# A transformer block on one Trainium2 core: the up weights of two chunks split by transfers instead of by engines, and 24 products into an unread bank at the end

## The chip, the cores and the metric

One core of a Trainium2 chip runs the whole program. The metric is device microseconds of one execution, here the median of the runs; the profile is of one more execution, and its times are counted from its first instruction.

## The reference

One layer: attention, then a feed-forward block with squared ReLU, each between two RMS norms, on 256 tokens of width 1024 in float32. The change touches the feed-forward block alone.

```python
def squared_relu_mlp(x, w_up, w_down):
    return jnp.square(jax.nn.relu(x @ w_up)) @ w_down

h = h + rms_norm(moba_attention(rms_norm(h, g1), w_qkv, w_o), g2)
u = squared_relu_mlp(rms_norm(h, g3), w_up, w_down)      # w_up [1024, 4096], w_down [4096, 1024]
h = h + rms_norm(u, g4)
```

## The kernel before

**Split weights.** Every float32 weight is split into two float32r parts, hi (rounded to 12 bits) and lo (the rest, weight minus hi). A product of float32 matrices is three products of parts (`mm3`, L209 to L214): hi by hi (L212), hi by lo (L213) and lo by hi (L214). In the up products the weight is the stationary operand: L212 and L213 use its hi part, L214 its lo part.

**The stream of pieces.** `Weights` (L28 to L99) cuts all weights into 48 pieces of 128 partitions by 2048 columns (1 MB) in the order of their use. Here the pieces that matter are, by number: up2 22 and 23, down1 24 and 25, up3 26 and 27, down2 28 and 29, up4 30 and 31, down3 32 and 33, up5 34 and 35. `load` (L45) issues one load into one of five raw buffers from the SP queue. `pump` (L71) splits: for one of the four steps of a piece ACT writes a quarter of hi (L83) and DVE the same quarter of lo (L84). Each of the tags whi and wlo has four buffers, so that piece i takes the parts buffer of piece i-4, and a step of piece i is only emitted when piece i-4 has been marked as used up by `done` (L75). When a piece's four steps are emitted, the next load is emitted.

**The feed-forward block.** For chunks c from 1 to 7 the loop at L669 runs `up_chunk(c)` (L645: four groups f of 24 products, eight row blocks k by three, 128x128 by 128x256; piece `up{c}` holds k 0 to 3 and its successor k 4 to 7) and `down_chunk(c - 1)` (L659: 48 products of 128x128 by 128x512). After each f two steps are pumped (L656, L667). The steps of an up piece begin to be emitted at the end of `up_chunk(c - 1)` (L655, L656).

**Order.** TensorE (PE) and the SP queue keep the order of the program (L113). ACT, DVE and POOL are put in order by the framework's scheduler, which goes by priority and by when it expects an operand to be ready; on the chip each engine then works strictly in that order. The last chunk's `down` products go by token tile, each followed by its norm and its two output transfers (L679 to L686).

Of the kernel before, what the change touches and what calls it, by code (L numbers as in the profile page):

```python
# [8 lines left out]
F32 = mybir.dt.float32  # L9
F32R = mybir.dt.float32r  # L10
BF16 = mybir.dt.bfloat16
AF = mybir.ActivationFunctionType
ALU = mybir.AluOpType
# [4 lines left out]
P = 128  # L18
HEADS = 8
EPS = 1e-6  # L20
# [5 lines left out]


class Weights:  # L28
    """Streams the weights through SBUF in pieces of [128, 2048] and splits each float32
    exactly into two float32r parts: hi (12 bits, rounded) and lo (the rest). A piece is split  # L30
    in four steps; step (i, j) is the j-th of piece i."""

    N = 2048

    def __init__(self, nc, raw_pool, part_pool, raw_bufs, part_bufs):
        self.nc, self.raw_pool, self.part_pool = nc, raw_pool, part_pool
        self.raw_bufs, self.part_bufs = raw_bufs, part_bufs
        self.sources, self.raw, self.parts, self.steps, self.split = [], {}, {}, [], set()
        self.loaded = self.finished = self.next = self.part = 0

    def add(self, src, how, cuts=1):
        self.sources.append((src, how, cuts))
        return len(self.sources) - 1

    def load(self, n=None):  # L45
        """The next n parts of a piece's load, by default all that remain."""
        i = self.loaded
        if i >= len(self.sources):
            return
        src, _, cuts = self.sources[i]  # L50
        k, c = src.shape[1], src.shape[2]
        if i not in self.raw:
            self.raw[i] = self.raw_pool.tile([P, k, c], F32, name=f"raw{i}", tag="raw", bufs=self.raw_bufs)
        n = n or cuts - self.part
        w = k // cuts
        for j in range(self.part, self.part + n):
            self.nc.sync.dma_start(self.raw[i][:, j * w:(j + 1) * w, :], src[:, j * w:(j + 1) * w, :])
        self.part += n
        if self.part == cuts:
            self.loaded += 1  # L60
            self.part = 0
# [9 lines left out]
    def pump(self, n, lo_engine=None):  # L71
        nc = self.nc
        while n > 0 and self.next < len(self.steps):
            i, j = self.steps[self.next]
            if i >= self.finished + self.part_bufs or i >= self.loaded:  # L75
                return
            if i not in self.parts:
                shape = list(self.raw[i].shape)
                self.parts[i] = [self.part_pool.tile(shape, F32R, name=f"w{p}{i}", tag=f"w{p}", bufs=self.part_bufs)
                                 for p in ("hi", "lo")]  # L80
            hi, lo = (self.slice(t, i, j) for t in self.parts[i])
            x = self.slice(self.raw[i], i, j)
            nc.scalar.activation(hi, x, AF.Copy)  # L83
            (lo_engine or nc.vector).tensor_tensor(lo, x, f32(hi), op=ALU.subtract)  # L84
            self.split.add((i, j))
            self.next += 1
            n -= 1
            if sum((i, q) in self.split for q in range(4)) == 4:
                self.load()
# [13 lines left out]
def block(ctx: ExitStack, tc: tile.TileContext, x, g_mix_pre, g_mix_post, g_ffn_pre, g_ffn_post,  # L103
          w_up, w_down, w_qkv, w_o, out):
    nc = tc.nc
    S, D = x.shape[1], x.shape[2]
# [12 lines left out]
    at = ctx.enter_context(tc.tile_pool(name="at", bufs=4, space=PSUM))  # L119

    def bank(pool, name):
        return pool.tile([P, 512], F32, name=name, tag="b")

    # ---- the weights in the order of their use
    wq = w_qkv[0].rearrange("(k p) c -> p k c", p=P)
    wo = w_o[0].rearrange("(k p) c -> p k c", p=P)
    wu = w_up[0].rearrange("(k p) c -> p k c", p=P)
# [2 lines left out]
    piece = {}  # L130

    def add_cols(name, w, c, how, cuts=1):
        """512 columns in two pieces of four row blocks"""
        i = piece[name] = W.add(w[:, 0:4, c:c + 512], how, cuts)
        W.add(w[:, 4:8, c:c + 512], how, cuts)
        if how == "cols":
            W.steps += [(i + e, j) for j in range(4) for e in range(2)]
        else:
            W.steps += [(i + e, j) for e in range(2) for j in range(4)]

    def add_rows(name, w, k):
        """four row blocks in two pieces"""
        i = piece[name] = W.add(w[:, k:k + 2, :], "rows")
        W.add(w[:, k + 2:k + 4, :], "rows")
        W.steps += [(i + e, j) for e in range(2) for j in range(4)]
# [10 lines left out]
    for c in range(NC):  # L156
        add_cols(f"up{c}", wu, 512 * c, "cols" if c else "k")
        if c > 0:
            add_rows(f"down{c - 1}", wd, 4 * (c - 1))
    add_rows(f"down{NC - 1}", wd, 4 * (NC - 1))  # L160

    # ---- loads: x's columns as the first weights need them
    xs = const.tile([P, NT, D], F32, name="xs")
    xv = x[0].rearrange("(t p) d -> p t d", p=P)
    grow = [const.tile([KT, P], F32, name=f"grow{i}") for i in range(2)]
# [15 lines left out]
    for name, g in (("mix", g_mix_post), ("ffn", g_ffn_post)):  # L181
        gb[name] = const.tile([P, D], F32, name=f"g_{name}")

    # ---- constants
    ident = const.tile([P, P], F32, name="ident")
    make_identity(nc, ident)
    one = const.tile([P, P], F32, name="one")
# [2 lines left out]
    nc.gpsimd.tensor_copy(ones, one)  # L190
    power = const.tile([P, 2], F32, name="power")
    nc.gpsimd.memset(power, -0.5)
    # distances of queries 128.. to keys 0..255, then of queries 0.. to keys 0..127
    dist = const.tile([P, 384], F32, name="dist")
    nc.gpsimd.iota(dist[:, 0:256], pattern=[[-1, 256]], base=P, channel_multiplier=1,
                   allow_small_or_imprecise_dtypes=True)
# [10 lines left out]
    oT = [const.tile([P, HEADS, S], F32R, name=f"oT{i}") for i in range(2)]  # L207

    def mm3(ps, a, b, start, stop):  # L209
        """ps (+)= (a0 + a1).T @ (b0 + b1) without the product of the low parts, which lies below  # L210
        a float32's rounding."""
        nc.tensor.matmul(ps, lhsT=a[0], rhs=b[0], start=start, stop=False)  # L212
        nc.tensor.matmul(ps, lhsT=a[0], rhs=b[1], start=False, stop=False)  # L213
        nc.tensor.matmul(ps, lhsT=a[1], rhs=b[0], start=False, stop=stop)  # L214
# [7 lines left out]
        nc.vector.scalar_tensor_tensor(dst[1], ps, scale, f32(dst[0]), op0=ALU.mult, op1=ALU.subtract)  # L222

    def square(junk, x, acc):
        """acc = the row sums of x * x / D"""
        nc.scalar.activation(junk, x, AF.Square, scale=D ** -0.5, accum_out=acc)

    def rstd_of(a, b, dst):
        """dst = (a + b + EPS) ** -0.5"""
        ms = small.tile(list(dst.shape), F32, name="ms")  # L230
        nc.vector.scalar_tensor_tensor(ms, a, EPS, b, op0=ALU.add, op1=ALU.add)
        nc.gpsimd.tensor_tensor(dst, ms, power[:, :dst.shape[1]], op=ALU.pow)

    def diag_of(rstd):
        """diagonal matrices of rstd, split in two parts"""
        dg = [small.tile([P, S], F32R, name=f"diag{i}", bufs=1) for i in range(2)]
        for t in range(NT):
            hi, lo = (a[:, t * P:(t + 1) * P] for a in dg)
            nc.vector.tensor_scalar(hi, ident, rstd[:, t:t + 1], None, op0=ALU.mult)
            nc.vector.scalar_tensor_tensor(lo, ident, rstd[:, t:t + 1], f32(hi), op0=ALU.mult, op1=ALU.subtract)  # L240
        return dg

    def row_of(dg, dst, pool):
        """dst[:, t] = rstd[t] on every partition"""
        ps = bank(pool, "psrow")
        for i in range(2):
            nc.tensor.matmul(ps[:, :S], lhsT=ones, rhs=dg[i], start=i == 0, stop=i == 1)
        nc.scalar.activation(dst, ps[:, :S], AF.Copy)

    # ---- x transposed, times the first gain; its rows' norms come in later  # L250
    banks = [bank(at, f"xt{j}") for j in range(4)]

    def transpose_x(k, t):
# [87 lines left out]
        nc.scalar.activation(hi, full, AF.Copy)  # L341
        nc.vector.tensor_tensor(lo, full, f32(hi), op=ALU.subtract)

    # ---- attention, a head at a time; the queries of the second half come first
    prob, probT = {}, {}
    cut = ((0, 256, 1), (256, 384, 0))

# [54 lines left out]
        W.pump(1, nc.gpsimd if h % 2 else None)  # L402
        (q_evac if kind == "q" else k_evac)(h, ps)

    # ---- values, queries and keys of the first heads
    idle = const.tile([P, 512], BF16, name="idle")
    psi = bank(mm, "psidle")

    def keep_busy(n):
        """products of zeros, which keep TensorE's clock up while it waits"""  # L410
        for _ in range(n):
            nc.tensor.matmul(psi, lhsT=idle[:, :P], rhs=idle, start=True, stop=True)

# [67 lines left out]
        if h == 3:  # L481
            transpose_p(4)

    # ---- projection of the heads' outputs
    acc = [[bank(mm, f"acc{t}_{c}") for c in range(2)] for t in range(NT)]

    def rows_unit(name, j, act, t, c, start, stop):
# [17 lines left out]
            transpose_p(h + 5)  # L505
        attend(h + 4)

    # ---- h = x + rms_norm(attention), over x; then transposed, times the next gain
    qk_pool.release()
    mlp = ctx.enter_context(tc.tile_pool(name="mlp", bufs=2, reuse_waits="tile"))  # L510
    yg = mlp.tile([P, NT, D], F32, name="yg", bufs=1)

    class PostNorm:
        """residual + rms_norm of a token tile of the accumulated rows"""

        def __init__(self, t, name):
            self.t, self.gain = t, gb[name]
# [21 lines left out]
            if late is not None and f == 0:  # L539
                late()  # L540

    # ---- the feed-forward block
    ssq2 = const.tile([P, 2, NT], F32, name="ssq2")
    rstd2 = const.tile([P, NT], F32, name="rstd2")
    rrow2 = const.tile([P, S], F32, name="rrow2")
# [11 lines left out]
        nc.scalar.activation(u, r, AF.Square)  # L557
        nc.vector.tensor_tensor(lo, u, f32(hi), op=ALU.subtract)  # L558

    # the first chunk goes by token tiles, its result being transposed: the first tile's products  # L560
    # run while the second one's norm is worked out
    rT = {}

    def up_first(t, k):
# [114 lines left out]
    for t in range(NT):  # L679
        norm = PostNorm(t, "ffn")  # L680
        for c in range(2):
            last_rows(f"down{NC - 1}", act_down, t, c)
            norm.take(c)
        for a, b in ((0, 512), (512, D)):
            norm.put(yg, a, b)
            nc.sync.dma_start(ov[:, t, a:b], yg[:, t, a:b])  # L686
    W.done(2)


# [23 lines left out]
```

## Time and profile before

| | us |
|---|---|
| median of 2 runs | 307.49 (306.96 to 308.01) |
| span of the profiled execution | 304.8 |
| PE busy in it | 295.1 (97%) |
| DVE busy | 194.1 (64%) |
| ACT busy | 166.6 (55%) |
| POOL busy | 24.4 (8%) |

The span runs from the first to the last instruction that the profiler recorded; the run's time is 2.7 us longer. A product that PE runs is shown with the time from its start to its modelled end, and these overlap: the pace of products is read from one start to the next. In a timeline a line is start, duration, engine, line of the kernel, operation, output<-input and count, and in brackets the idle time of the engine before it and what ended it.

### The profile page before, as it was taken

Reading aid. Unit: us, or ns where it says so; the run is one execution under the profiler, and the core shown is the slowest. Engines: PE = TensorE matmul, PEld = TensorE weight load, DVE = VectorE, ACT = ScalarE, POOL = GpSimd, SP = SyncE. Lnnn points to the kernel's source line nnn. Section 1 sums busy time; section 2 is a strip of 40 time slices with the busy share of each in tenths; the row PEclk is TensorE's granted clock in tenths of the full one; section 3 lists DMA queues with packets and bytes.
Section 4 is the critical chain, followed back from the end, with each engine's and each line's share of the span. In section 5 each row is a group of like instructions: output and inputs, shape, how many; then the busy total and the mean of one; then the engine's idle time right before and its main releaser. Section 6 shows DMA issues by size and latency. Waiting matters only on the chain.

```text
span 304.8 us, 4862 instructions
## 1 busy us (share of the span) xinstructions
PE 295.1 (97%) x1838; PEld 261.9 (86%) x1838; DVE 194.1 (64%) x403; ACT 166.6 (55%) x395; POOL 24.4 (8%) x38
## 2 busy tenths in 40 slices
PE   8999999999999989999999999999999999999991
PEld 4689999988998868898898898898898898898880
DVE  3569989774688296899448447447447447547042
ACT  4777938765393365987437427427527526526020
POOL 4000224002200072000000000000000000000000
PEclk9999999999999999999999999999999999999998
DMA  6998694739405234078970860960960950300012
GB/s 201 374 387 310 205 380 172 251 133 347 141 3 166 110 138 140 0 254 293 298 261 1 310 245 0 326 226 2 336 214 9 345 199 12 129 0 3 0 57 80
DMA packets 22055, 53.79 MB, mean 176 GB/s; under 512 B 1024, under 2 KB 1552, under 8 KB 22032
## 3 DMA queue, kind: packets, MB, share of 16 engines
q1 hardware_dynamic: 22032, 53.49, 50.1%
q8 instruction: 14, 0.23, 0.3%
q14 instruction: 9, 0.07, 0.1%
HBM read 52.44 MB, written 1.05 MB: 175 GB/s over the span
## 4 chain that ended last, share of the span: by engine, by line
PE 80%; issue 10%; DVE 5%; DMA 2%; SPq 1%; ACT 1%; POOL 1%; DVEq 0%; POOLq 0%
PE psu L212 10%; PE psu L214 10%; PE psu L213 10%; PE acd L213 9%; PE acd L212 9%; PE acd L214 9%; PE psq L212 3%; PE psq L213 3%; PE psq L214 3%; DVE wlo L84 2%; PE psv L292 2%; PE psv L294 2%; PE psv L296 2%; DMA raw<-in_attn_w_qkv_dram 2%; PE psk L212 1%
## 5 line engine op out<-in xcount | busy, mean ns | idle before, releaser
L84 DVE TENSOR_TENSOR wlo<-raw,whi 128x512 fp32r<-128x512 f32 x182 | 118.3, 697 | 43.2 <-ACT whi L83 43.0
L83 ACT ACTIVATE whi<-raw 128x512 fp32r<-128x512 f32 x192 | 107.0, 623 | 46.4 <-PE acd L214 33.3
L212 PE MATMUL psu<-xT,whi 128*128 128x256 f32 x224 | 63.4, 283 | 0.0
L213 PE MATMUL psu<-xT,whi 128*128 128x256 f32 x224 | 63.3, 282 | 0.0
L214 PE MATMUL psu<-xT,wlo 128*128 128x256 f32 x224 | 62.9, 281 | 0.0
L213 PE MATMUL acd<-wlo,uhi 128*128 128x512 f32 x128 | 50.5, 395 | 0.0
L212 PE MATMUL acd<-whi,uhi 128*128 128x512 f32 x128 | 50.5, 395 | 0.0
L214 PE MATMUL acd<-whi,ulo 128*128 128x512 f32 x128 | 50.5, 394 | 0.0
L214 PEld LDWEIGHTS psu<-xT,wlo 128*128 128x128 f32 x224 | 42.5, 190 | 0.0
L213 PEld LDWEIGHTS psu<-xT,whi 128*128 128x128 f32 x224 | 42.1, 188 | 0.3
L212 PEld LDWEIGHTS psu<-xT,whi 128*128 128x128 f32 x224 | 41.9, 187 | 0.3
L556 ACT ACTIVATE uhi<-r 128x256 fp32r<-128x256 f32 x28 | 11.6, 413 | 35.0 <-DVE r L555 35.0
L214 PEld LDWEIGHTS acd<-whi,ulo 128*128 128x128 f32 x128 | 24.1, 188 | 5.6
L212 PEld LDWEIGHTS acd<-whi,uhi 128*128 128x128 f32 x128 | 24.1, 188 | 5.4
L213 PEld LDWEIGHTS acd<-wlo,uhi 128*128 128x128 f32 x128 | 24.1, 189 | 5.3
L558 DVE TENSOR_TENSOR ulo<-u,uhi 128x256 fp32r<-128x256 f32 x28 | 11.8, 423 | 14.4 <-ACT u L557 14.4
L555 DVE SCALAR_TENSOR_TENSOR r<-psu,rrow 128x256 f32<-128x256 f32 x28 | 11.7, 419 | 13.7 <-PE psu L214 13.7
L212 PE MATMUL psq<-xT,whi 128*128 128x256 f32 x64 | 18.4, 288 | 0.0
L212 PE MATMUL psk<-xT,whi 128*128 128x256 f32 x64 | 18.4, 287 | 0.0
L529 POOL TENSOR_TENSOR rs<-mss,power 128x1 f32<-128x1 f32 x4 | 2.2, 550 | 198.6 <-DVE mss L527 198.6
L214 PE MATMUL psq<-xT,wlo 128*128 128x256 f32 x64 | 18.1, 282 | 0.0
L213 PE MATMUL psq<-xT,whi 128*128 128x256 f32 x64 | 18.0, 282 | 0.0
(121 smaller groups left out, 455.2 us busy)
## 6 DMA issues: line engine op xcount, KB each, us to landing
raw<-in_w_up_dram SPq DMA_DIRECT2D x16, 1024.0 KB, 5.6
raw<-in_w_down_dram SPq DMA_DIRECT2D x16, 1024.0 KB, 7.5
raw<-in_attn_w_qkv_dram SPq DMA_DIRECT2D x10, 1024.0 KB, 8.6
raw<-in_attn_w_o_dram SPq DMA_DIRECT2D x4, 1024.0 KB, 5.7
raw<-in_attn_w_qkv_dram SPq DMA_DIRECT2D x8, 256.0 KB, 6.3
out_dram<-yg SPq DMA_DIRECT2D x4, 256.0 KB, 2.0
xs<-in_x_dram SPq DMA_DIRECT2D x2, 256.0 KB, 4.9
xs<-in_x_dram SPq DMA_DIRECT2D x1, 512.0 KB, 7.1
```

Of the source, the lines that this page charges most:

```text
L83: nc.scalar.activation(hi, x, AF.Copy)
L84: (lo_engine or nc.vector).tensor_tensor(lo, x, f32(hi), op=ALU.subtract)
L212: nc.tensor.matmul(ps, lhsT=a[0], rhs=b[0], start=start, stop=False)
L213: nc.tensor.matmul(ps, lhsT=a[0], rhs=b[1], start=False, stop=False)
L214: nc.tensor.matmul(ps, lhsT=a[1], rhs=b[0], start=False, stop=stop)
L292: nc.tensor.matmul(psv[0][t], lhsT=x0[t], rhs=w[0], start=first, stop=False)
L294: nc.tensor.matmul(psv[0][t], lhsT=x1[t], rhs=w[0], start=False, stop=False)
L296: nc.tensor.matmul(psv[0][t], lhsT=x0[t], rhs=w[1], start=False, stop=last)
L529: nc.gpsimd.tensor_tensor(self.rs, ms, power[:, :1], op=ALU.pow)
L555: nc.vector.scalar_tensor_tensor(r, ps[:, :S], 0.0, rrow2, op0=ALU.max, op1=ALU.mult)
L556: nc.scalar.activation(hi, r, AF.Square)
L558: nc.vector.tensor_tensor(lo, u, f32(hi), op=ALU.subtract)
```

## The change

The two pieces each of up3 (26 and 27) and up5 (34 and 35) are marked (`W.rounded`). For a marked piece `load` issues nothing and only counts it as loaded. At its first step `pump` emits three things: a load of the whole 1 MB from memory into hi, issued from the POOL queue, which rounds on its way; one ACT instruction that writes lo as minus hi, 128x2048; and a second load of the same 1 MB from the POOL queue that adds onto lo. The other steps of the piece emit nothing. So lo becomes weight minus hi, and its ACT and DVE steps and its SP load are gone. At the very end of the program 24 products are emitted on PE into a bank that nobody reads: six each of bf16 zeros by 512 columns, of the last down piece's hi part read as bf16 by 512 columns, of the same as float32r by 512, and as float32r by 256 columns. The removed comments leave empty lines and change nothing.

```diff
@@ class Weights
+        self.rounded, self.started = set(), 0
+    def by_dma(self, i):
+        return i in self.rounded
     def load(self, n=None):
         src, _, cuts = self.sources[i]
+        if self.by_dma(i):
+            self.loaded += 1
+            return
@@ pump
             if i not in self.parts:
-                shape = list(self.raw[i].shape)
+                shape = list(self.sources[i][0].shape)
                 self.parts[i] = [self.part_pool.tile(shape, F32R, name=f"w{p}{i}", tag=f"w{p}", bufs=self.part_bufs)
                                  for p in ("hi", "lo")]
+            if self.by_dma(i):
+                if (i, -1) not in self.split:
+                    self.split.add((i, -1))
+                    (hi, lo), src = self.parts[i], self.sources[i][0]
+                    nc.gpsimd.dma_start(hi, src)
+                    nc.scalar.activation(lo, hi.bitcast(F32), AF.Copy, scale=-1.0)
+                    nc.gpsimd.dma_start(lo, src, accum_op=ALU.add)
+                self.split.add((i, j))
+                self.next += 1
+                n -= 1
+                if sum((i, q) in self.split for q in range(4)) == 4:
+                    self.load()
+                continue
             hi, lo = (self.slice(t, i, j) for t in self.parts[i])
@@ the list of pieces
         add_cols(f"up{c}", wu, 512 * c, "cols" if c else "k")
         if c > 0:
+            if c in (3, 5):
+                W.rounded |= {piece[f"up{c}"], piece[f"up{c}"] + 1}
             add_rows(f"down{c - 1}", wd, 4 * (c - 1))
@@ the end
+    tail = bank(at, "pstail")
+    hi, lo = W.parts[piece[f"down{NC - 1}"]]
+    for n, (a, b) in enumerate(((idle[:, :P], idle), (hi.bitcast(BF16)[:, 0, 0:P], hi.bitcast(BF16)[:, 1, 0:512]),
+                                (hi[:, 0, 0:P], hi[:, 1, 0:512]), (hi[:, 0, 0:P], hi[:, 1, 0:256]))):
+        for _ in range(6):
+            nc.tensor.matmul(tail[:, :b.shape[-1]], lhsT=a, rhs=b, start=True, stop=True)
     W.done(2)
```

## Rows read from the trace of the kernel before

**Rows 1.** The page: busy shares, then the chain that ended last, by engine.

```profile
PE 295.1 (97%) x1838; PEld 261.9 (86%) x1838; DVE 194.1 (64%) x403; ACT 166.6 (55%) x395; POOL 24.4 (8%) x38
...
PE 80%; issue 10%; DVE 5%; DMA 2%; SPq 1%; ACT 1%; POOL 1%; DVEq 0%; POOLq 0%
```

**Rows 2.** Timeline of PE, the end of up_chunk(2).

```profile
160.85 0.29 PE L213 MATMUL psu<-xT,whi 128*128 128x256 f32 x1
160.98 0.28 PE L214 MATMUL psu<-xT,wlo 128*128 128x256 f32 x1
...
162.42 0.28 PE L214 MATMUL psu<-xT,wlo 128*128 128x256 f32 x1
162.54 0.40 PE L212 MATMUL acd<-whi,uhi 128*128 128x512 f32 x1
162.77 0.40 PE L213 MATMUL acd<-wlo,uhi 128*128 128x512 f32 x1
```

**Rows 3.** Timeline of PE, the start of up_chunk(3).

```profile
173.69 0.28 PE L212 MATMUL psu<-xT,whi 128*128 128x256 f32 x1
173.81 0.29 PE L213 MATMUL psu<-xT,whi 128*128 128x256 f32 x1
173.93 0.30 PE L214 MATMUL psu<-xT,wlo 128*128 128x256 f32 x1
...
175.13 0.28 PE L212 MATMUL psu<-xT,whi 128*128 128x256 f32 x1
```

**Rows 4.** Timeline of ACT, from up_chunk(2) to the start of up_chunk(3).

```profile
161.18 2.72 ACT L83 ACTIVATE whi<-raw 128x512 fp32r<-128x512 f32 x5
163.80 0.40 ACT L556 ACTIVATE uhi<-r 128x256 fp32r<-128x256 f32 x1
164.11 0.40 ACT L557 ACTIVATE u<-r 128x256 f32<-128x256 f32 x1
164.41 1.66 ACT L83 ACTIVATE whi<-raw 128x512 fp32r<-128x512 f32 x3
168.32 2.19 ACT L83 ACTIVATE whi<-raw 128x512 fp32r<-128x512 f32 x4 [2.25 <-PE acd L214]
173.89 2.19 ACT L83 ACTIVATE whi<-raw 128x512 fp32r<-128x512 f32 x4 [3.37 <-PE acd L214]
```

**Rows 5.** The page's groups of the split: busy, mean ns, idle before.

```profile
L84 DVE TENSOR_TENSOR wlo<-raw,whi 128x512 fp32r<-128x512 f32 x182 | 118.3, 697 | 43.2 <-ACT whi L83 43.0
L83 ACT ACTIVATE whi<-raw 128x512 fp32r<-128x512 f32 x192 | 107.0, 623 | 46.4 <-PE acd L214 33.3
```

**Rows 6.** Timeline of DVE: the last lo parts of up3.

```profile
164.95 2.49 DVE L84 TENSOR_TENSOR wlo<-raw,whi 128x512 fp32r<-128x512 f32 x4
```

**Rows 7.** Transfers in 154.2 to 160.2, a load alone: rate in 40 slices, then issue to landing.

```profile
GB/s 382 355 300 109 82 27 27 27 137 191 150 164 109 96 205 191 205 273 328 328 423 437 423 423 355 423 423 369 396 355 259 178 191 55 14 0 0 0 0 0
...
raw<-in_w_up_dram SPq DMA_DIRECT2D x1, 1024.0 KB, 5.4
```

**Rows 8.** Transfers in 166 to 176, three loads that overlap: issue to landing.

```profile
raw<-in_w_down_dram SPq DMA_DIRECT2D x2, 1024.0 KB, 7.7
raw<-in_w_up_dram SPq DMA_DIRECT2D x1, 1024.0 KB, 5.6
```

**Rows 9.** Stretches: length, then busy us (count) of PE, PEld, DVE, ACT, POOL, clock, DMA share, GB/s.

```profile
160.00:170.00 10.00, 10.00 (x56) 8.59 (x55) 7.32 (x14) 7.30 (x16) 0.00 (x0) 1.00 0.17 46
172.00:173.00 1.00, 1.00 (x5) 0.78 (x5) 0.00 (x0) 0.00 (x0) 0.00 (x0) 1.00 1.05 430
```

**Rows 10.** Timeline of the SP queue, loads 30 to 33 and 34.

```profile
154.41 12.83 SPq L57 DMA_DIRECT2D raw<-in_w_up_dram  x2
167.47 4.41 SPq L57 DMA_DIRECT2D raw<-in_w_down_dram  x2
177.08 12.84 SPq L57 DMA_DIRECT2D raw<-in_w_up_dram  x2
```

**Rows 11.** The costliest POOL instruction of the split (groups by form).

```profile
L84 POOL TENSOR_TENSOR wlo<-raw,whi 128x512 fp32r<-128x512 f32 x10 | 14.0, 1413 | 36.6 <-ACT whi L83 36.5
```

**Rows 12.** Timeline of the end: the last product and the last issues of output.

```profile
297.98 0.40 PE L214 MATMUL acd<-whi,ulo 128*128 128x512 f32 x1
...
300.85 0.99 SPq L686 DMA_DIRECT2D out_dram<-yg  x2
```

**Rows 13.** Stretches after the last product, columns as in rows 9.

```profile
301.00:302.00 1.00, 0.00 (x0) 0.00 (x0) 0.49 (x1) 0.00 (x0) 0.00 (x0) 1.00 0.30 119
302.00:303.00 1.00, 0.00 (x0) 0.00 (x0) 0.00 (x0) 0.00 (x0) 0.00 (x0) 0.90 1.01 393
303.00:304.00 1.00, 0.00 (x0) 0.00 (x0) 0.00 (x0) 0.00 (x0) 0.00 (x0) 0.50 0.04 12
```

**Rows 14.** Timeline of PE at the program's start: bf16 products of zeros.

```profile
1.17 2.31 PE L412 MATMUL psidle<-idle 128*128 128x512 bf16 x5 [1.17 <-DVE idle L415]
```

## Prediction

> **What bounds the kernel now.** I read the busy shares and the chain of waits first [rows 1]: PE is busy for 97% of the span and carries 80% of the chain, the other engines have a third or more of it free. In the feed-forward block PE is paced by its own products: in the up products one starts every 0.12 us, in the down products every 0.23 us [rows 2, 3]. The reader should then look at who delivers to PE around the changed place, the start of up_chunk(3). Its pieces 26 and 27 are split by ACT in 161.18 to about 166.1 [rows 4] and by DVE until 164.95 + 2.49 = 167.44 [rows 6], while PE asks for them at 173.69 [rows 3]. So there are 6.2 us of slack, and faster splitting buys nothing. The same pattern returns in each chunk, 22.7 us apart, so what holds for up3 holds for up5. What counts is whether the new way still delivers by 173.7.
>
> **What is removed.** Four pieces lose four steps each: 16 ACT instructions of 0.623 us (10.0 us) and 16 DVE instructions of 0.697 us (11.2 us) [rows 5], and four SP loads. None lay on PE's path (6.2 us of slack), so I take 0 for all of it. A gain is excluded: PE starts a product at its pace without a hole on both sides of the seam [rows 2, 3].
>
> **What is added before up_chunk(3), and when it can start.** The rounding load of piece 26 writes a hi buffer that piece 22 held. Its last reader is the L213 product at 160.85, for lo the L214 at 160.98 [rows 2]; so it can go at about 161.2. Piece 27 takes piece 23's buffers, free after the product at 162.42, about 162.6. ACT's order speaks for it that waiting is for exactly this: five of the eight steps of these pieces start at 161.18 [rows 4]. From there a chain of four things runs for each piece: load, negation, adding load, PE.
>
> *The load.* A plain load of 1 MB alone on the queue took 5.4 us from issue to landing [rows 7]. At full flow the engines move 0.43 MB/us [rows 9], so 2.4 us of these are moving and 3.0 us are start and landing; in the row of rates nothing much flows in the first and the last of them [rows 7]. No transfer of POOL's is in this trace. For its issue I bound what comes on top by 0 and by POOL's 1.41 us for an elementwise instruction [rows 11], and take 1.0. For rounding I take nothing. SP's loads are no rival in this stretch: 30 was issued at 154.41, 31 only at about 166.9 and 32 at 167.47 [rows 10], each when an older raw buffer came free; with two pieces fewer in the ring of five these go earlier still, and 160 to 170 had a DMA share of only 0.17 [rows 9]. So hi of 26 lands at 161.2 + 1.0 + 5.4 = 167.6, hi of 27, both moving 2.1 MB, at 161.2 + 1.0 + 3.0 + 4.9 = 170.1.
>
> *The negation.* Five 512-column instructions of ACT in a row take 2.72 us [rows 4], 0.54 each, so 2048 columns take 2.2 us at most. 26 is ready at 169.8, 27 at 172.3. Behind them on ACT wait the steps of down2 (2.19 us at 168.32 and at 173.89 [rows 4]); these parts are needed 11.2 us after up_chunk(3) begins, so a few us late costs nothing.
>
> *The adding load.* No row shows one. Lower bound: a plain load. Upper bound: each 1 MB flows four times as slowly. To add, the old value must be read too, so I take twice the bytes, 4.9 us of flow for each piece. Both together: 169.8 + 1.0 + 3.0 + 9.8 = 183.6. SP's load 33 follows the split of piece 28 and falls into it, 2.4 us of flow; I take half, 1.2. lo of 27 lands at 184.8.
>
> The Trainium skill (DMA: Bandwidth & Descriptors, SDMA does more than copy) says that the add unit reduces two streams elementwise; no run here shows its rate. With one stream's bytes instead the above would end at 178.7, and the kernel at about 315.
>
> *PE.* L214 of the third product waits for lo of 26 (173.93), and after twelve products L212 of k = 4 for 27 (175.13 [rows 3]); the L214 two products later is the last. The chunk goes on at 184.8 instead of 175.4 at the latest: some 9.5 us late. Everything on PE is queued behind it; ACT, DVE and the SP loads follow PE, so nothing is made up later, and up5 pays the same again: 19.0 us.
>
> *The clock.* After its last product (ending about 298.4) PE's granted clock stayed at 1.00 to the stretch of 302 and was 0.50 (the lower level, 1.2 GHz) from 303 [rows 12, 13]. [...] At the start of the program five bf16 products took 2.31 us, 0.46 each [rows 14], twice the 0.23 of 512 columns in the block. Bounds per wait: 0, and one group of 24 products at half pace, 2.9 us; I take 1.5, so 3.0 for two.
>
> **The 24 products at the end.** PE's last product ends at about 298.4, the last output transfers are issued at 300.85 to 301.8 [rows 12], and the span ends at 304.8: 6.4 us in which PE does nothing. At 0.23 us for 512 columns and 0.12 for 256, 18 and 6 products are 4.9 us: hidden under the last norm and output, with 1.5 us left. If that cover were gone they would cost 4.9; at the pace of rows 14 they would take up to 11.0 and stand out by 4.6. They follow straight on busy products, so I take 0.
>
> **Sum.** 0 (removed) + 19.0 + 3.0 + 0 = 22.0 us. The profiled execution has a span of 304.8 and would go to 326.8; its run lies 2.7 us above its span, and the median of the runs is 307.5, so 329.5.
>
> **The rivals.**
>
> *The transfers fit (the other side).* Nothing for POOL's issue, the adding load as fast as a plain one: hi of 27 at 162.6 + 5.4 = 168.0, ACT until 170.9 at the latest (26 first, at 166.6), lo of 27 at 176.3. That is about 1 us late, twice: 309.5, within 2%. Speaking for it: transfers have the queue to themselves in 160 to 170 [rows 9]. Against it: two loads that overlapped took 7.7 us [rows 8]. It decides as long as lo of 27 lands before 178.5 (2% is 6.1 us, 3.1 for each chunk). Chance 0.14.
>
> The Trainium skill (DMA: Bandwidth & Descriptors, Anatomy of one DMA) gives a fit for transfers issued from POOL, 2.0 us plus bytes by 436 GB/s. That is an estimate of 4.4 us for 1 MB; with it lo of 27 would land at about 174 and the kernel stay at 307.5. The only loads in this trace, SP's, took 5.4 [rows 7].
>
> *Adding at the plain rate, with POOL's cost and sharing.* lo at 178.7, 3.3 to 4 us late each time, no drop of the clock: 315. Chance 0.15.
>
> *The hi load of 27 is queued behind the adding load of 26.* POOL works in order. Were it put in the program's order, its second instruction would wait for the negation until 169.8, and only then could hi of 27 be issued: 169.8 + 1.0 + 3.0 + 7.3 (three streams) = 181.1, negated 183.3, added 183.3 + 1.0 + 3.0 + 4.9 = 192.2. That is 17 us late, twice, with the clock 37: 344. Against it: ACT's steps of 26 and 27, which alternate in the program, ran 26's before 27's when 26's buffers came free first [rows 4], so the scheduler goes by readiness. Chance 0.15. A rounding load at half the rate gives some 5 us more each, 340, and is counted here.
>
> *The adding load is much slower.* Four times: 19.6 us of flow for both, 169.8 + 4.0 + 19.6 + 2.4 = 195.8, 20.5 us late, twice, and the clock: 351. Chance 0.12.
>
> **How the numbers follow.** The forecast (one wait of 7 to 11 us at each of the two chunks, 321 to 337) has 0.42. Fits 0.14, plain rate 0.15, order or rounding 0.15, very slow 0.12; for faster than before by over 2% nothing speaks, 0.02 is left. About 2% is what a measurement of this kernel tells from no change. Slower is 0.42 + 0.15 + 0.15 + 0.12 = 0.84, same 0.14. For 8 in 10 the range leaves out about half of the fitting case and most of the slowest: 311 to 348. The likeliest case's own range is 321 to 337.
>
> **What would show it.** In the profile after: L83 176 times and L84 on DVE 166 times; POOL issuing eight transfers; two holes in PE, in front of L214 psu at the third product and again twelve products later, in the third and the fifth up chunk and in no other, with DMA as what ended them. hi lands before 173.7 and lo after: then the adding load is the late one. If the first hole stands ahead of L212, hi was late. If POOL's second hi load is issued after an adding load, the order was the cause. The end must show 24 products that finish before the output lands. The forecast is wrong if PE has no hole, if the holes are there but below 3 us each, or if up_chunk(4) or a down chunk waits as well.

## Result and profile after

The changed kernel takes 338.93 us (338.74 to 339.11), the kernel before 307.49: a ratio of 1.103, with a 95% interval of 1.100 to 1.107. The profiled execution has a span of 337.3 us.

The start of a profile, up to the first query products, moves by up to 2.4 us from one profile here to another. Where two profiles are compared below, I use the stretch from the first product of up_chunk(1) to the start of the last down product, and call it the block's stretch. Before: 127.93 to 297.98, 170.05 us. After: 128.85 to 330.61, 201.76 us. So 31.7 us were lost in it, and from the last product to the span's end it is 6.7 us after and 6.8 before.

The page of the changed kernel: the group of L238 (L214 before) with its idle time, and the transfers of POOL (size, median time from issue to landing).

```profile
PE 307.1 (91%) x1862; PEld 271.8 (81%) x1862; DVE 185.1 (55%) x387; ACT 165.8 (49%) x383; POOL 32.9 (10%) x46
...
L238 PE MATMUL psu<-xT,wlo 128*128 128x256 f32 x224 | 66.2, 295 | 25.0 <-DMA wlo<-in_w_up_dram 25.0
...
whi<-in_w_up_dram POOLq DMA_DIRECT2D x4, 1024.0 KB, 6.6
wlo<-in_w_up_dram POOLq DMA_DIRECT2D x4, 1024.0 KB, 12.2
```

PE is busy for 91% of the span instead of 97% [rows 1]: it now waits 25.0 us for lo, in four waits, two in up_chunk(3) and two in up_chunk(5). No other chunk has a wait. Its timeline at the start of up_chunk(3) answers to [rows 3]; the seam lies 0.92 us later in this execution, at 174.61 instead of 173.69.

```profile
174.61 0.28 PE L236 MATMUL psu<-xT,whi 128*128 128x256 f32 x1
174.73 0.28 PE L237 MATMUL psu<-xT,whi 128*128 128x256 f32 x1
179.18 0.58 PE L238 MATMUL psu<-xT,wlo 128*128 128x256 f32 x1 [4.17 <-DMA wlo<-in_w_up_dram]
179.56 0.41 PE L236 MATMUL psu<-xT,whi 128*128 128x256 f32 x1
...
181.69 0.41 PE L237 MATMUL psu<-xT,whi 128*128 128x256 f32 x1
190.82 0.58 PE L238 MATMUL psu<-xT,wlo 128*128 128x256 f32 x1 [8.72 <-DMA wlo<-in_w_up_dram]
191.20 0.42 PE L236 MATMUL psu<-xT,whi 128*128 128x256 f32 x1
191.42 0.41 PE L237 MATMUL psu<-xT,whi 128*128 128x256 f32 x1
```

Both hi products run on time and the first lo product stands still; the same twelve products later. Undisturbed, the second of these lo products would have come 14 products of 0.12 us after the seam, at 176.29: it is 14.5 us late. In up_chunk(5) the two waits are 4.0 and 8.1 us, and that product is 13.8 us late. Behind each wait the products come every 0.213 us instead of 0.12, at a granted clock of 0.50. Of the 31.7 us, 28.3 are these two delays; the other 3.4 are lost behind the second wait of each chunk. POOL's and ACT's timelines show the chain that PE waits for.

```profile
162.40 1.00 POOL L94 DMA_DIRECT2D whi<-in_w_up_dram  x1 [35.89 <-PE psu L238]
163.83 0.76 POOL L94 DMA_DIRECT2D whi<-in_w_up_dram  x1 [0.43 <-PE psu L238]
170.78 1.31 POOL L96 DMA_DIRECT2D wlo<-in_w_up_dram  x1 [6.19 <-ACT wlo L95]
174.15 1.28 POOL L96 DMA_DIRECT2D wlo<-in_w_up_dram  x1 [2.06 <-ACT wlo L95]
```

```profile
168.56 1.92 ACT L95 ACTIVATE wlo<-whi 128x2048 fp32r<-128x2048 f32 x1 [3.71 <-DMA whi<-in_w_up_dram]
170.39 1.66 ACT L105 ACTIVATE whi<-raw 128x512 fp32r<-128x512 f32 x3
171.95 1.90 ACT L95 ACTIVATE wlo<-whi 128x2048 fp32r<-128x2048 f32 x1
```

The second adding load is issued at 174.15 and its product starts at 190.82, 16.7 us later. In that time the transfer engines are full, but at a low rate. Stretches of the changed kernel, columns as in [rows 9] (the last one, 194 to 195, shows the clock coming back), then SP's transfers in 160 to 200:

```profile
173.00:179.00 6.00, 2.02 (x10) 1.50 (x8) 3.19 (x5) 3.56 (x6) 1.28 (x1) 0.84 1.08 186
...
177.00:178.00 1.00, 0.00 (x0) 0.00 (x0) 0.97 (x2) 0.01 (x1) 0.00 (x0) 0.51 1.13 207
...
179.00:189.30 10.30, 2.93 (x12) 2.63 (x12) 0.00 (x0) 0.00 (x0) 0.00 (x0) 0.50 1.04 291
...
194.00:195.00 1.00, 1.00 (x10) 1.00 (x10) 0.42 (x1) 0.55 (x2) 0.00 (x0) 0.96 0.00 0
...
raw<-in_w_down_dram SPq DMA_DIRECT2D x2, 1024.0 KB, 13.0
```

Plain loads with full engines moved 430 GB/s [rows 9]; here it is 186 at first and 291 later. Two things share it: the adding loads of 26 and 27 (2.1 MB) and SP's loads 33 and 36, issued at 175.1 and 178.0 (2.1 MB, 12.3 and 13.6 us to landing).

### The profile page after: what moved, and what is told of

It is laid out like the page before. It is cut to its first block, busy times and chain, and to the rows that moved or that the text cites. A ratio compares the mean times of both kernels' runs of the same rounds, so it can differ in the third digit from the quotient of the medians.

```text
span 337.3 us, 4891 instructions
## 1 busy us (share of the span) xinstructions
PE 307.1 (91%) x1862; PEld 271.8 (81%) x1862; DVE 185.1 (55%) x387; ACT 165.8 (49%) x383; POOL 32.9 (10%) x46
## 5 line engine op out<-in xcount | busy, mean ns | idle before, releaser
L106 DVE TENSOR_TENSOR wlo<-raw,whi 128x512 fp32r<-128x512 f32 x166 | 108.5, 701 | 48.0 <-ACT whi L105 47.8
L105 ACT ACTIVATE whi<-raw 128x512 fp32r<-128x512 f32 x176 | 98.5, 624 | 36.2 <-PE acd L238 23.0
L238 PE MATMUL psu<-xT,wlo 128*128 128x256 f32 x224 | 66.2, 295 | 25.0 <-DMA wlo<-in_w_up_dram 25.0
L238 PEld LDWEIGHTS psu<-xT,wlo 128*128 128x128 f32 x224 | 45.1, 201 | 26.1 <-DMA wlo<-in_w_up_dram 26.1
L236 PE MATMUL psu<-xT,whi 128*128 128x256 f32 x224 | 65.9, 294 | 0.0
L237 PE MATMUL psu<-xT,whi 128*128 128x256 f32 x224 | 65.7, 293 | 0.0
L236 PE MATMUL acd<-whi,uhi 128*128 128x512 f32 x128 | 50.5, 395 | 0.0
L238 PE MATMUL acd<-whi,ulo 128*128 128x512 f32 x128 | 50.5, 394 | 0.0
L580 ACT ACTIVATE uhi<-r 128x256 fp32r<-128x256 f32 x28 | 11.7, 417 | 71.0 <-DVE r L579 71.0
L237 PEld LDWEIGHTS psu<-xT,whi 128*128 128x128 f32 x224 | 44.8, 200 | 0.3
L236 PEld LDWEIGHTS psu<-xT,whi 128*128 128x128 f32 x224 | 44.8, 200 | 0.3
L238 PEld LDWEIGHTS acd<-whi,ulo 128*128 128x128 f32 x128 | 24.1, 188 | 5.6
L236 PEld LDWEIGHTS acd<-whi,uhi 128*128 128x128 f32 x128 | 24.1, 188 | 5.4
L236 PE MATMUL psq<-xT,whi 128*128 128x256 f32 x64 | 18.4, 288 | 0.0
L236 PE MATMUL psk<-xT,whi 128*128 128x256 f32 x64 | 18.4, 287 | 0.0
L238 PE MATMUL psq<-xT,wlo 128*128 128x256 f32 x64 | 18.1, 282 | 0.0
L238 PE MATMUL psk<-xT,wlo 128*128 128x256 f32 x64 | 18.0, 282 | 0.0
## 6 DMA issues: line engine op xcount, KB each, us to landing
wlo<-in_w_up_dram POOLq DMA_DIRECT2D x4, 1024.0 KB, 12.2
```

What stands on the lines that cost most here:

```text
L580: nc.scalar.activation(hi, r, AF.Square)
```

## The experiments

**1. The second load overwrites instead of adding.**

```diff
-                    nc.gpsimd.dma_start(lo, src, accum_op=ALU.add)
+                    nc.gpsimd.dma_start(lo, src)
```

> The second load of each marked piece no longer adds, it overwrites (lo holds the rounded weight, so the addition is left out). Theory A, the adding itself is the price (it moves more than twice a plain load's time per byte): the four second loads land about 7 us after their issue instead of 8.4 and 16.6, lo of 27 at about 181 instead of 190.8, 5.5 us late instead of 14.5, PE's clock hardly falls: 319 to 322 us. Rival B, these transfers are slow because SP's loads 33 and 36 run beside them, whatever they do: lo of 27 not before 187, 330 us or more.

Measured: 317.04 us, block's stretch 179.42 us (+9.4 over the kernel before). Page and PE's timeline of this run:

```profile
wlo<-in_w_up_dram POOLq DMA_DIRECT2D x4, 1024.0 KB, 5.8
```

```profile
177.09 0.39 PE L238 MATMUL psu<-xT,wlo 128*128 128x256 f32 x1 [1.79 <-DMA wlo<-in_w_up_dram]
...
180.45 0.58 PE L238 MATMUL psu<-xT,wlo 128*128 128x256 f32 x1 [0.88 <-DMA wlo<-in_w_up_dram]
```

The same transfers at the same place, with SP's loads beside them, land after 5.8 us when they don't add. The time is a little below the range of theory A, and far from B. Issuing from POOL and rounding are not what is slow: 9.4 us of the 31.7 is the chain of two plain loads that doesn't fit the lead, and 22.3 us comes with the adding, the time that SP's loads and the lower clock then add to it included.

**2. SP's loads held back until lo has landed.**

```diff
+        if i in (33, 41):
+            held = self.raw_pool.tile([P, 4], F32, name=f"held{i}", tag="held", bufs=2)
+            self.nc.sync.dma_start(held, f32(self.parts[i - 6][1][:, 0, 0:4]))
```

> SP's loads 33 and 41 (and all that follow on SP) wait until the lo part of piece 27 (35) has landed, by a 2 KB transfer ahead of them on SP that reads it; everything else as in the changed kernel. Theory B, the share that two 1 MB loads take: 4.9 us of flow at 0.43 MB/us is given back, lo of 27 lands at about 186, some 5 us sooner at each of the two chunks: 328 to 330 us. Theory A alone (the adding transfers are limited by themselves): 337 to 339 us.

Measured: 325.02 us, 13.9 less than the changed kernel and more than I had expected. The reason for the excess is in experiments 11 and 12: the small tile `held` alone makes the up products faster. What the gate is worth is told there. The run's own value is the rate of adding with the engines to itself (stretch, and PE's timeline):

```profile
172.00:181.50 9.50, 4.05 (x18) 3.39 (x16) 3.19 (x5) 2.73 (x6) 1.28 (x1) 0.72 1.11 204
```

```profile
177.50 0.58 PE L241 MATMUL psu<-xT,wlo 128*128 128x256 f32 x1 [4.38 <-DMA wlo<-in_w_up_dram]
...
182.56 0.58 PE L241 MATMUL psu<-xT,wlo 128*128 128x256 f32 x1 [2.13 <-DMA wlo<-in_w_up_dram]
```

The engines are full (1.11) and move 204 GB/s, half of the 430 that plain loads reach [rows 9]. The first wait is as long as in the changed kernel (4.38 and 4.17 us), the second is 2.13 instead of 8.72: SP's loads lengthen the second one only.

**3. One piece of each chunk by transfers.**

```diff
-                W.rounded |= {piece[f"up{c}"], piece[f"up{c}"] + 1}
+                W.rounded |= {piece[f"up{c}"]}
```

> Only the first piece of each of the two chunks (26 and 34) goes by transfers, the second (27 and 35) by ACT and DVE as before. If the second hole and the lower clock came only from two adding loads side by side, one hole of 2.5 to 4.3 us is left in each chunk, without a drop of the clock: 312 to 316 us. If an adding load is slow by itself whatever runs beside it, lo of 26 lands 8.4 us after its issue as before, 4.3 us late twice: 316 us; with half of the loss per piece, as a loss that goes by the number of pieces: 323 us.

Measured: 322.57 us, block's stretch 186.51 (+16.5). That is the last of the three numbers, half of the loss with half of the pieces: a single adding load is no shorter a wait than the first of two. PE's timeline, both chunks:

```profile
179.82 0.58 PE L238 MATMUL psu<-xT,wlo 128*128 128x256 f32 x1 [5.46 <-DMA wlo<-in_w_up_dram]
...
234.57 0.58 PE L238 MATMUL psu<-xT,wlo 128*128 128x256 f32 x1 [7.76 <-DMA wlo<-in_w_up_dram]
```

The two loads took 9.7 and 12.1 us to land, with two SP loads running beside each of them. That the second hole came only from two adding loads side by side has fallen.

**4. One piece, with SP's loads held back** (experiments 2 and 3 together, with SP waiting ahead of loads 32 and 40).

> Only the first piece of each chunk (26 and 34) by transfers, in the ring's buffers, and SP's loads from 32 (40) on wait until lo of 26 (34) has landed. This is one adding load with the engines to itself: at the half rate that the gated pair showed (205 GB/s) 1.05 MB take 5.1 us of flow plus about 3 us, 8.2 us from issue to landing instead of 9.7 to 12.1; PE waits once for about 4 us in each chunk, too short to lower its clock: 315 to 317 us. If the 5.5 and 7.8 us waits of the ungated run come from the adding itself and not from SP's loads: 321 to 323 us.

Measured: 317.02 us. The adding load takes 8.4 us in both chunks:

```profile
wlo<-in_w_up_dram POOLq DMA_DIRECT2D x2, 1024.0 KB, 8.4
```

```profile
173.00:174.00 1.00, 0.00 (x0) 0.00 (x0) 0.79 (x2) 1.00 (x3) 0.00 (x0) 1.00 1.13 207
...
175.00:176.00 1.00, 0.00 (x0) 0.00 (x0) 0.71 (x2) 0.00 (x0) 0.00 (x0) 0.62 1.09 201
176.00:177.00 1.00, 0.10 (x1) 0.10 (x1) 0.00 (x0) 0.00 (x0) 0.00 (x0) 0.50 0.16 27
```

So a lone adding load of 1 MB flows at 201 to 207 GB/s and costs 8.4 us from issue to landing, against 5.8 for one that overwrites (experiment 1). One part of the expectation was wrong: with waits of 4.2 and 3.9 us the clock did go down, from 1.00 to 0.62 in 175 to 176 and to 0.50 behind it, with PE's last product started at 172.47. That the time still stands at the edge of the range is luck. The tile `held` makes this kernel faster too (experiment 11), and beside the kernel before with the same tile its block lost 181.20 - 168.01 = 13.2 us, of which 8.0 are the two waits and 4.7 the 24 and 23 products behind them that start every 0.21 instead of 0.12 us.

**5. PE kept busy through the waits.**

```diff
+                if c in (3, 5) and f == 0 and k % 4 == 0:
+                    if k == 0:
+                        fill = bank(at, f"psfill{c}")
+                    for _ in range(44 if k else 19):
+                        nc.tensor.matmul(fill, lhsT=idle[:, :P], rhs=idle, start=True, stop=True)
```

> The changed kernel with bf16 products of zeros into an unread bank in front of the first and the thirteenth product of up_chunk(3) and up_chunk(5), 19 and 44 of them (0.216 us each, 4.1 and 9.5 us), so that PE works while lo is on its way. If the lower clock costs what its rows show behind the second wait (15 and 18 products at 0.213 instead of 0.12 us, 1.4 and 1.7 us), 335 to 336.5 us. If the clock costs nothing that the waits don't hide: 338 to 339.5; if the filling products push on the following ones: above 339.5.

Measured: 335.28 us, block's stretch 198.33 (3.4 less than 201.76), and a granted clock of 1.00 all through. Behind the filling PE's products are back at full pace at once:

```profile
190.07 0.38 PE L238 MATMUL psu<-xT,wlo 128*128 128x256 f32 x1 [0.17 <-DMA wlo<-in_w_up_dram]
190.29 0.28 PE L236 MATMUL psu<-xT,whi 128*128 128x256 f32 x1
190.41 0.29 PE L237 MATMUL psu<-xT,whi 128*128 128x256 f32 x1
```

From the landing of the second lo to the end of the chunk it is now 10.0 us instead of 11.4 and 11.7: the lower clock cost 3.1 us for both chunks. The remaining 0.3 us is mostly that the second lo lands a little sooner in this run (15.9 and 15.3 us after the end of the down products ahead of it, instead of 16.2 and 15.5).

**6. Pieces of w_down instead of w_up: lines of 4 KB, and a lead of 17 us.**

```diff
-            if c in (3, 5):
-                W.rounded |= {piece[f"up{c}"], piece[f"up{c}"] + 1}
             add_rows(f"down{c - 1}", wd, 4 * (c - 1))
+            if c in (3, 5):
+                W.rounded |= {piece[f"down{c - 1}"], piece[f"down{c - 1}"] + 1}
```

> The same three steps for down2 and down4 (28, 29, 36, 37) instead of up3 and up5: lines of 4 KB instead of 2 KB in memory, and a lead of 17 us instead of 12 from the free buffer to the first use. Theory, the chain takes 16 to 22 us with SP's loads beside it and half the rate while it adds: lo of 28 lands about 1 us late, lo of 29 in time or up to 4 us late, 308 to 316 us; the adding transfers flow at about 205 GB/s alone here too. Rival, the rate of adding goes by the number of lines and not by bytes: near 400 GB/s with 4 KB lines and no wait at all, 307.5.

Measured: 313.66 us, block's stretch +8.0. The two changed down chunks took 13.67 and 16.67 us instead of 11.15. Rate in 40 slices of 180 to 192, where SP's queue moved 0.03 MB:

```profile
GB/s 0 0 0 205 68 41 109 55 218 218 218 218 218 218 177 218 218 218 218 218 218 218 205 137 137 191 218 191 191 177 218 218 177 218 205 205 218 218 205 219
```

218 GB/s with lines of 4 KB, 205 with 2 KB: the price of adding goes by bytes and not by the number of lines. The loss is a quarter of 31.7; it isn't gone. The lead alone doesn't make that quarter: from the issue of the first hi load to the chunk's first product it is 16.6 us instead of 12.2, but in a down chunk PE also asks for the second piece only 24 products of 0.23 us after the first, and not twelve of 0.12. One wait per chunk is left, for the first lo (PE's timeline), and in the second of these chunks the granted clock was 0.63 in 237 to 241:

```profile
187.28 0.50 PE L237 MATMUL acd<-wlo,uhi 128*128 128x512 f32 x1 [2.13 <-DMA wlo<-in_w_down_dram]
...
236.68 0.50 PE L237 MATMUL acd<-wlo,uhi 128*128 128x512 f32 x1 [3.68 <-DMA wlo<-in_w_down_dram]
```

**7. Without the 24 products.** (The edit deletes the block that begins with `tail`.)

> The changed kernel without the 24 products at its end. If they lie under the last norm and output, as their end 1 us before the span's suggests: the same as with them, 338 to 340 us. If the end of the program waits for them: 1 to 5 us less.

Measured: 337.67 us, with an interval of the ratio of 1.095 to 1.103 beside 1.100 to 1.107. That is just under the range of the first case, but the two intervals overlap, and in its profile the block began 1.9 us sooner; its block's stretch is 201.61 instead of 201.76, and the time from the start of the last down product to the end 6.74 instead of 6.72. The products cost nothing. They end in time in the changed kernel (timeline of PE; the span ends at 337.3):

```profile
330.61 0.40 PE L238 MATMUL acd<-whi,ulo 128*128 128x512 f32 x1
330.85 1.47 PE L716 MATMUL pstail<-idle 128*128 128x512 bf16 x6
332.15 3.56 PE L716 MATMUL pstail<-whi 128*128 128x512 bf16 x18
```

**8. One piece, in buffers that are free early.** As in experiment 3 only the first piece of each chunk goes by transfers. Pieces 26 and 34 take the tiles oT, unused once the heads' outputs are projected, and are emitted ahead of up_chunk(1) and up_chunk(4).

```diff
+    def ahead(self, i, tiles):
+        nc = self.nc
+        self.parts[i] = [t.rearrange("p (k a) s -> p k (a s)", a=2) for t in tiles]
+        self.split.add((i, -1))
+        (hi, lo), src = self.parts[i], self.sources[i][0]
+        nc.gpsimd.dma_start(hi, src)
+        nc.scalar.activation(lo, hi.bitcast(F32), AF.Copy, scale=-1.0)
+        nc.gpsimd.dma_start(lo, src, accum_op=ALU.add)
...
     for c in range(1, NC):
+        if c in (1, 4):
+            W.ahead(piece["up3" if c == 1 else "up5"], oT)
         up_chunk(c)
```

> As the run with one piece, but hi and lo of 26 (34) lie in the two tiles oT, which are free from the first up chunk on, and the transfers are issued one to two stages earlier. Theory, the lead time alone is what is missing (the buffer comes free 12 us ahead of its use and the chain takes 16 to 18): no hole in PE, 307 to 309 us. Rival, the transfers, the negation at its place in ACT's order, or the shared DMA engines hold up something else as well: 311 us or more.

Measured: 310.05 us, between the two. From up_chunk(1) on there is no wait, the block's stretch is 169.92 us; but ahead of it PE waits, since ACT does (timeline of ACT):

```profile
123.39 1.92 ACT L116 ACTIVATE oT<-oT 128x2048 fp32r<-128x2048 f32 x1 [3.11 <-DMA oT<-in_w_up_dram]
```

The scheduler had put the negation into the norm between two evacuations, with the hi load still on its way. PE waits 0.84 and 0.85 us there. The lead was enough; the place in ACT's order cost 2 to 3 us.

**9. The same, emitted ahead of up_chunk(2)** (`if c in (2, 4)`).

> As the run with one piece ahead in the tiles oT, but the transfers of 26 are emitted before up_chunk(2) instead of before up_chunk(1). In the run before, the two new waits of PE were at 125.6 (0.84 us, behind ACT) and 127.4 (0.85 us, behind DVE), where the negation waited 3.1 us on ACT for the hi load in the middle of the norm. Theory, that place in ACT's order is the whole rest: no wait of PE in the block, 307.0 to 308.0 us, same as before. Rival, the adding load beside SP's loads costs PE something wherever it stands: 309.5 us or more again.

Measured: 309.83 us. The expectation was wrong, and the row says why: the transfers of 26 had not moved. oT is free just as early, and the scheduler goes by that.

```profile
123.38 1.91 ACT L116 ACTIVATE oT<-oT 128x2048 fp32r<-128x2048 f32 x1 [2.96 <-DMA oT<-in_w_up_dram]
```

**10. The same, with a true dependence.**

```diff
+        if c in (2, 4):
+            for t in oT:
+                nc.vector.tensor_copy(t[:, 0, 0:1], up[c - 1][0][:, 0, 0:1])
             W.ahead(piece["up3" if c == 2 else "up5"], oT)
```

> As the run with one piece ahead in oT, before up_chunk(2) and up_chunk(4), but one-column VectorE copies from the parts of the chunk before into both tiles go ahead of the transfers, so that they can't start before that chunk's first group is done (about 131 and 177 us). The run before had lost 2.0 us ahead of up_chunk(1): the scheduler had put the negation into the norm all the same, since oT was free from 115.7, and ACT waited 2.96 us there for the hi load. Theory: with the negation out of the norm no wait of PE is left; 307.0 to 308.0 us, the same as before. Rival, the adding load beside PE and SP's loads costs something wherever it stands: 309 us or more.

Measured: 305.80 us over 11 runs, beside 307.50 over 15 of the kernel before: a ratio of 0.9967 by the means (0.9944 to 0.9990). No wait of PE is left; the block's stretch is 169.92 us against 170.05. So two pieces by transfers cost nothing when their buffers come free a stage sooner and ACT isn't made to wait in the norm. The last 0.3%, 1.0 us, are accounted for in part: the block gives 0.1 us of them, the stretch behind it 0.3 (6.54 instead of 6.83 us); the rest stays open.

**11 and 12. A shift of 32 bytes.** In experiments 2 and 4, and in no others, the up chunks without a wait took 11.21 us instead of 11.52. Both have the tile `held`, twice 16 bytes per partition. Here it is added alone, to the kernel before and to the changed one; POOL fills it once, at 2.7 us, and nobody reads it.

```diff
+        if i in (33, 41):
+            held = self.raw_pool.tile([P, 4], F32, name=f"held{i}", tag="held", bufs=2)
+            self.nc.gpsimd.memset(held, 0.0)
```

> The kernel before with two tiles of 16 bytes per partition in the pool of the raw buffers, filled once by POOL and not read: nothing else changes but the address of what lies behind that pool (the weight parts among it), by 32 bytes. In the two runs in which SP waited for a small tile, the up chunks that have no wait took 11.21 us instead of the 11.52 of all other runs, a product every 0.117 instead of 0.120 us. Theory, the small tile's shift of the addresses does it: 11.21 us for each of six up chunks here too, and the same share in the query and key products: 303.5 to 305 us. Rival, it came from SP's waiting and the calmer transfers: 11.52 us and 307 to 308 us.

> The changed kernel with the same two small tiles, and no waiting on SP. It is what the run with the gate has to be measured against. If the tiles' shift is what quickens the up products: 2.2 us less from the first up chunk to the last product and some 3 to 3.5 us less in all, 335 to 336.5 us, so that the gate itself gave back about 11 us and not 13.9. If it came from the gate: 338 to 339.5 us.

Measured: the kernel before goes from 306.69 to 304.19 us, a ratio of 0.9922 (0.9901 to 0.9943); it is the fastest kernel of this study. All its undisturbed up chunks take 11.20 to 11.21 us, and the query and key products too come every 0.117 us; down chunks stay at 11.14 to 11.20. No trace shows an address: that the shift is the reason is argued from the edit, which adds to the program only these two tiles and 0.14 us of POOL. Timeline of PE at the same seam as [rows 3], a product every 0.117 us on average instead of 0.120:

```profile
173.52 0.28 PE L215 MATMUL psu<-xT,whi 128*128 128x256 f32 x1
...
175.86 0.28 PE L217 MATMUL psu<-xT,wlo 128*128 128x256 f32 x1
```

The second of these rows is 20 products behind the first. The changed kernel with the tile takes 334.27 us, somewhat below the range of the theory, block's stretch 197.49; with the gate as well it was 187.95. So the gate, that is SP's loads beside the adding loads, is worth 9.5 us, less than the 11 expected: 5.3 in up_chunk(3) (26.56 to 21.25 us) and 4.2 in up_chunk(5) (25.35 to 21.18). Counted from the start of the chunk, the second lo lands 4.6 and 3.9 us later beside SP's loads than without them; the rest comes with the longer wait, as products at the lower clock. Two plain loads need 2.1 MB / 0.43 MB/us = 4.9 us of the engines. The waits of up_chunk(3) without the gate (PE's timeline; with it they are 4.38 and 2.13 us, experiment 2):

```profile
177.08 0.58 PE L241 MATMUL psu<-xT,wlo 128*128 128x256 f32 x1 [4.33 <-DMA wlo<-in_w_up_dram]
...
186.74 0.58 PE L241 MATMUL psu<-xT,wlo 128*128 128x256 f32 x1 [6.73 <-DMA wlo<-in_w_up_dram]
```

## Why the prediction was right, and what it sized wrong

The direction, the mechanism and the range were right: 338.9 in 311 to 348, where 329.5 was named. It lies just beyond the likeliest case's own 321 to 337: there a wait of 7 to 11 us at each chunk was named, and the two waits of a chunk came to 12.9 and 12.1. The range alone would have been weak support. It was 37 us wide and also held the plain rate (315) and the wrong order (344), so that the order on POOL, the rate of adding and the overwriting run decide, not the number.

- *What is removed is worth nothing.* Right: PE had no wait there before, and none of the other chunks got faster by it (11.52 and 11.15 us in the changed kernel too). In experiment 10 the removal for two of the four pieces gives 0.1 us in the block.
- *Start and hi load.* Right. The seam taken off (0.92 us), the loads are issued at 161.5 and 162.9 instead of 161.2 and 162.6, and the negation of 26 starts at 167.6, as worked out. No hole stands ahead of L236: hi was in time in both chunks. POOL's part in it is 0.76 to 1.00 us, near the 1.0 taken.
- *The negation.* 1.91 us instead of 2.2. That of 27 stood behind three splits of 28 on ACT and ended at 172.9 instead of 172.3.
- *The rate of adding.* The term that no row of before showed was right in size: twice the flow of a plain load. 204 to 218 GB/s with full engines is half of 430. That reading the old value is the reason was argued, and no run separates it from another cause of half the rate. With SP's loads out of the way the block lost 187.95 - 168.01 = 19.9 us against the kernel before with the same small tile; the sum without its term for SP's loads was 2 x 8.3 + 3.0 = 19.6. The parts agree too: the product that waits for the second lo was 8.2 us late in both chunks. The rival with the plain rate was also priced well, 315 against 317.04 in experiment 1.

The Trainium skill (DMA: Bandwidth & Descriptors, SDMA does more than copy) describes the add as two streams that are reduced. The half rate, 204 to 218 against 430 GB/s, agrees with that reading. For a transfer from POOL the Trainium skill (DMA: Bandwidth & Descriptors, Anatomy of one DMA) gives 2.0 us and bytes by 436 GB/s, for 1 MB an estimate of 4.4 us. That doesn't hold here: a rounding load from POOL that ran alone took 5.8 to 6.0 us (experiment 4), two that overlapped 6.0 to 7.3 in the changed kernel.

- *SP's loads beside it: the step that was mis-sized.* "SP's load 33 follows the split of piece 28 and falls into it, 2.4 us of flow; I take half, 1.2." It was two loads, 33 and 36, since the split of 29 frees its raw buffer at 178.0, when lo was still on its way; [rows 10] had it to see, there SP issues load 34 at 177.08, the same place in the chunk. And they took nearly their whole share: lo landed 4.6 and 3.9 us later by them, and the chunks became 5.3 and 4.2 us longer instead of 1.2 each (experiments 2 and 12). That is 9.5 us instead of 2.4, and makes up 7.1 of the 9.4 us between 329.5 and 338.9. The rest stays open in part. By the profiles the changed kernel loses 31.7 us where its twin with the small tile loses 29.5 (197.49 - 168.01), 2.2 us more; by the medians of the runs it is 31.4 and 30.1, and the twin's two runs lie 2.1 us apart, the profiled one being the faster.
- *The clock.* 3.0 us in the sum, 3.1 measured (experiment 5). Part of the low clock is covered: the twelve slow products between the waits cost nothing, as the second wait would only have been longer. Where no second wait covers them, in experiment 4, the slow products cost 2.4 and 2.3 us.
- *The 24 products.* Right: hidden, ended 1.6 us ahead of the span's end, 0.1 us of difference without them (experiment 7).
- *The rivals.* POOL's order was hi, hi, lo, lo, by readiness. Rounding doesn't slow a load: the two hi loads moved 396 GB/s in 166 to 170 in the changed kernel, near the 430 of plain loads. Four times the bytes, no: 204 to 218 GB/s are half of the plain rate.
- *The run and its span.* "its run lies 2.7 us above its span" (and the table of before with it) sets the median of other runs against the span of one profile. The profiled run of the changed kernel took 339.11 us with a span of 337.3, 1.8 more. The forecast doesn't change by it, since the 22.0 us are added to the median.

## To carry to other kernels

A load that adds kept the transfer engines here for twice the time of a plain one (204 to 218 against 430 GB/s), and what another queue issued meanwhile came on top almost in full (3.9 and 4.6 of 4.9 us); before such a chain is put on a ring of buffers, add up the time from the buffer's release to its first use and the flow of every queue in that stretch. A chain that is too long for the ring needs a buffer that is free sooner, and its engine instruction needs a true dependence that keeps it out of a place where that engine can't wait. Compare a stretch inside the kernel, not whole spans, and watch whether an edit has shifted addresses.

## What was not expected of the hardware

- Two unread tiles, 32 bytes per partition in front of the weight parts, took the up products from 0.120 to 0.117 us, 2.5 us of the whole kernel (experiments 11 and 12), and left the down products at 11.14 to 11.20 us a chunk. Which of the operands counts, and which addresses are good, wasn't tried; with piece 26 in oT, up_chunk(3) took 11.46 us in experiment 10, in between.
- PE's granted clock went down sooner than I had read from the kernel's end [rows 13]: 0.51 (near the lower level of 1.2 GHz) already in 177 to 178, after a last product started at 174.73. It stayed at 0.50 through twelve products between the waits and was back at 1.00 (2.4 GHz) by 195, with products running again from 190.82.
- In the changed kernel POOL needs 1.28 to 1.31 us to issue an adding load of 512 lines and 0.76 for a rounding one (1.00 for the first).
